# The hi parts of the input projection's weights cast by GpSimd, and the other arithmetic of the token mixing on VectorE and ScalarE

## The chip, the cores and the metric

The kernel runs on one core of a Trainium2 chip. The core has TensorE (matrix products; its weight loads are counted apart), VectorE and GpSimd (both elementwise), ScalarE (elementwise with a function), and DMA queues, most of them issued by SyncE. The metric is the device time of one execution in microseconds (us). A profile is one further execution, recorded by the hardware; its times can differ from the median by some tenths of a per cent.

## The reference, cut to what matters

A trunk of two layers over 1024 tokens of width 1024, in float32. Each layer has a norm with modulation, one input projection that two head groups share (differential attention, and an RWKV-7 recurrence), one output projection, and a mixture of experts:

```python
for l in range(DEPTH):
    h = rms_norm(x, norm1_g[l]) * (1.0 + sc1) + sh1
    proj = h @ w_in[l]
    q, k, v = ...                                   # group A: 4 heads, two softmax maps each
    attn_out = diff_attention(q, k, v, ...)
    rwkv_out = rwkv7_time_mix(proj[..., 3 * AW:], ...)   # group B: delta-rule state scan
    mixed = jnp.concatenate([attn_out, rwkv_out], axis=-1) @ w_out[l]
    x = x + gt1 * mixed
    h2 = rms_norm(x, norm2_g[l]) * (1.0 + sc2) + sh2
    x = x + gt2 * hier_moe(h2, ...)
return rms_norm(x, final_g)
```

## The kernel before, in words

Float32 products are made from three passes of TensorE's faster fp32r type. An operand is split in a hi part (rounded to fp32r) and a lo part (the operand less its hi), and the product is hi x hi + lo x hi + hi x lo. So each tile of weights costs a cast and a two-input subtract on some elementwise engine before TensorE can use it.

The stages of a layer follow one another, with their times in the profile: the first norm (to about 45 us in layer 0, 1385 to 1450 in layer 1); the mixing stage, `phase_a`, up to 905 and from 1450 to 2200; output projection and routing up to 1040 and 2320; the experts up to 1385 and 2690; the final norm.

In the mixing stage several generators are woven together:

- The input projection: `split_w` (L339) loads one of 25 weight tiles per layer by DMA into `wa_raw` (one buffer), casts it to `wa_hi`, subtracts to `wa_lo` (two buffers each). The first two tiles of a layer are cast by VectorE; the other 23 by ScalarE, through `wtile` (L439). `proj_cm` (L351) then makes 16 x 3 matmuls per tile for two halves of the tokens (L359 to L361).
- The recurrence: `rwkv_first` (L621), 4 pairs of heads by 4 quarters of the tokens. Its `chain` computes, mostly on VectorE, the decay `P` (L652), the products `bk` (L665, L666), and with GpSimd their scaled copies `bkb` (L669) and `arv[:, 0]` (L670, the identity scaled), each multiplied by the decay at the end of each chunk of 64 tokens, `pend`. TensorE multiplies them (`aa`, L681), transposes them (`tp`, L692), ScalarE copies the transposes out, VectorE masks `z` (L685). Then comes a triangular solve on VectorE (L748, L750), and the state scan `rwkv_back` (L866 on), whose bonus `b_bo` is a GpSimd product (L879), and `rwkv_last`, which norms a half and applies its scale and shift by three GpSimd operations (L931 to L933).
- The attention: `load_head` (L1073) splits q and k of a head, with ScalarE casts and GpSimd subtracts (L1092, L1097); then scores, softmax (`at_p`, L1178; the factors L1185, L1186; the difference L1187), transposes (L1196) and `at_o` (L1205).
- `out_weights` (L1220): 8 tiles of the output projection's weights per layer, each multiplied by the gate (VectorE, L1232), cast by ScalarE (L1233), its lo part subtracted by GpSimd (L1234).

The order on each engine is not the written one: a scheduler with its own model of durations takes the recorded instructions and lays each engine's row out, and the weaving adds due times. Each engine then runs its row in order. So an instruction that waits holds everything behind it on its engine.

Of the kernel before, what the change touches and what calls it, by code (L numbers as in the profile page):

```python
# [10 lines left out]
F32 = mybir.dt.float32  # L11
# [3 lines left out]
AF = mybir.ActivationFunctionType  # L15
OP = mybir.AluOpType
# [36 lines left out]
class Trunk:  # L53
# [285 lines left out]
    def split_w(self, wp, l, i, eng=None):  # L339

        nc = self.nc
        raw = wp.tile([128, NK, 128], F32, name="wa_raw", tag="wa_raw", bufs=1)
        nc.sync.dma_start(raw, self.a["w_in"][l, i])
        hi = wp.tile([128, NK, 128], F32R, name="wa_hi", tag="wa_hi")
        lo = wp.tile([128, NK, 128], F32R, name="wa_lo", tag="wa_lo")
        (eng or nc.vector.tensor_copy)(hi, raw)  # L346
        nc.gpsimd.tensor_tensor(lo, raw, hi.bitcast(F32), op=OP.subtract)  # L347
        return hi, lo


# [68 lines left out]
    def phase_a(self, l, x_src, psum, here, there):  # L419

        nc, a, tc = self.nc, self.a, self.tc
# [3 lines left out]
        wp, wl1, wk = self.wA, self.wl1, self.wk  # L425
# [11 lines left out]
                                   *(self.modulation(j, range(12), wpool, work, psum, 2) for j in range(1, L)))  # L437

        def wtile(c0):  # L439
            return self.split_w(wp, l, c0 // 128, eng=nc.scalar.copy)  # L440

        def lora():
            l1 = ring()
# [177 lines left out]
    def rwkv_first(self, hp, rp, ep, psum, krv, l2, w_up, a_up, sp):  # L621

        nc = self.nc
# [20 lines left out]
        def chain(q):  # L644
            k, r, v = (x[:, H * q:H * q + H] for x in krv)
# [3 lines left out]
            arv, bkb, bk = tl("arv", [128, 4, 4, 64]), tl("bkb", [128, 2, 4, 64]), tl("bk", [128, 2, 4, 64])  # L649
# [15 lines left out]
            nc.vector.tensor_mul(bk[:, 0], v3(ta), v3(u))  # L665
            nc.vector.tensor_mul(bk[:, 1], v3(th), v3(u))  # L666
            nc.scalar.copy(arv[:, 3], v3(v))
            for j in range(2):
                nc.gpsimd.tensor_tensor(bkb[:, j], bk[:, j], pend.to_broadcast([128, 4, 64]), op=OP.mult)  # L669
            nc.gpsimd.tensor_tensor(arv[:, 0], self.id2[:, None, :].to_broadcast([128, 4, 64]), pend.to_broadcast([128, 4, 64]), op=OP.mult)  # L670
            return arv, bkb, bk, rk

        def products(q, bk, arv, z):
# [190 lines left out]
    def rwkv_back(self, hp, q, t, pool, psum):  # L864
# [10 lines left out]
        if r == 0:  # L875
            self.bo = pool.tile([128, 4, 128], F32, name="b_bo", tag="b_bo")
            self.yh = pool.tile([128, 4, 128], F32, name="b_y", tag="b_y", bufs=2)
        bs = self.bsum[:, hp, 2 * q:2 * q + 2].rearrange("p t h -> p (t h)").unsqueeze(2).to_broadcast([128, 4, 64])
        nc.gpsimd.tensor_tensor(self.bo[:, r:r + 2].rearrange("p t (h n) -> p (t h) n", h=2), e[:, 1].rearrange("p t (h n) -> p (t h) n", h=2),  # L879
                                bs, op=OP.mult)  # L880
        hs = [slice(64 * h, 64 * h + 64) for h in range(2)]
        first = 0
# [33 lines left out]
    def rwkv_last(self, hp, half, y, bo, pool, psum):  # L916
# [11 lines left out]
        nc.vector.tensor_tensor(y3, y3, rs.unsqueeze(2).to_broadcast([128, 8, 64]), op=OP.mult)  # L928
        cs = slice(128 * hp, 128 * hp + 128)
        lnx = self.lnx  # L930
        nc.gpsimd.tensor_tensor(y, y, lnx[:, 0].unsqueeze(1).to_broadcast([128, 4, 128]), op=OP.mult)  # L931
        nc.gpsimd.tensor_tensor(bo, bo, lnx[:, 1].unsqueeze(1).to_broadcast([128, 4, 128]), op=OP.add)
        nc.gpsimd.tensor_tensor(y, y, bo, op=OP.add)  # L933

        def gate():
            ps = psum.tile([128, 4, 128], F32, name="rb_gt", tag="rb")
# [136 lines left out]
    def load_head(self, h):  # L1073
# [11 lines left out]
        for j, m, x in ((1, 0, tile("q0", F32)), (1, 1, tile("q1", F32)), (0, 0, tile("v", F32)), (0, 1, stage.tile([128, T], F32, name="st", tag="st"))):  # L1085
            for r in halves:
                nc.sync.dma_start(x[r], self.heads[h, j][halves[m]])
            if j:
                ks.append(tile(f"k{m}"))
                kl.append(tile(f"l{m}"))  # L1090
                nc.scalar.copy(ks[m], x)
                nc.gpsimd.tensor_tensor(kl[m], x, ks[m].bitcast(F32), op=OP.subtract)  # L1092
            else:
                dst = tile(f"q{m}")
                qs.append(dst)
                nc.scalar.copy(dst, x)
                nc.gpsimd.tensor_tensor(dst[64:128], x[64:128], dst[64:128].bitcast(F32), op=OP.subtract)  # L1097
        v = tile("v", F32).rearrange("p (t n) -> p t n", n=128)
        self.stacks[h] = (qs, ks, kl, v)
        nc.sync.dma_start(v, self.heads[h, 2])  # L1100
# [119 lines left out]
    def out_weights(self, l, k, wp, gate, keep):  # L1220
# [10 lines left out]
                      for n in names[2 * k:2 * k + 2])  # L1231
        nc.vector.tensor_tensor(raw, raw, gate, op=OP.mult)  # L1232
        nc.scalar.copy(hi, raw)  # L1233
        nc.gpsimd.tensor_tensor(lo, raw, hi.bitcast(F32), op=OP.subtract)  # L1234
        self.wo[k] = hi, lo

    def open_output(self, l, x_src, side):
# [736 lines left out]
```

## Time and profile before

| | us |
|---|---|
| Three timed runs | 2727.2, 2728.67, 2737.83 |
| Median | 2728.67 |
| The profiled execution: its time, its span | 2742.43, 2740.6 |
| TensorE busy in the span | 2400.2 |
| VectorE busy | 1836.7 |
| ScalarE busy | 1131.5 |
| GpSimd busy | 711.9 |

The mean granted clock of TensorE in that execution is 0.912 of full. An engine counts as busy while it runs an instruction, and also while an instruction that has started stands still for some other engine; such a stretch shows as a duration longer than the form's usual one. Idle time is put down to the instruction whose end came last before the waiting one could start.

### The profile page before, as it was taken

The numbers are of one execution on the slowest core, as the hardware profiler recorded it, in microseconds if no ns is written. First come the engines' busy times: TensorE is split into PE (matmuls) and PEld (weight loads), VectorE is DVE, ScalarE is ACT, GpSimd is POOL, SyncE is SP. The second block draws the span as 40 slices with busy tenths as digits, with TensorE's granted clock in tenths as the row PEclk, the third lists the DMA queues.
The fourth block names the chain that finished last, engine by engine and source line by source line (L and its number), as shares of the span: only waits on it lengthen the run. The fifth ranks groups of instructions, "written<-read, shape, count | busy, mean of one in ns | idle before, by whom it ended". The sixth has DMA issues, their size and how long they took to land. (4 is left out here: it accounts for less than half of the span.)

```text
span 2740.6 us, 45306 instructions
## 1 busy us (share of the span) xinstructions
PE 2400.2 (88%) x17313; PEld 1836.5 (67%) x17313; DVE 1836.7 (67%) x3803; ACT 1131.5 (41%) x2020; POOL 711.9 (26%) x525
## 2 busy tenths in 40 slices
PE   5998989898979969999959888889986897999992
PEld 3676657687767866777737666667765786677771
DVE  3358875464658477877753689974648847787775
ACT  4333332244345225555544333324426422455552
POOL 4122221313141013333311222323314200233330
PEclk7999988798979979999979989889988897999996
DMA  8476675534272258999851434355426224899985
GB/s 286 159 233 222 177 218 155 155 115 132 88 218 70 96 193 303 355 336 368 309 213 47 155 107 150 113 153 156 136 76 204 73 89 180 303 384 352 335 311 200
DMA packets 262787, 542.68 MB, mean 198 GB/s; under 512 B 76376, under 2 KB 180768, under 8 KB 232608
## 3 DMA queue, kind: packets, MB, share of 16 engines
q1 hardware_dynamic: 234560, 484.61, 52.6%
q0 software_dynamic: 23376, 40.99, 4.0%
q10 hardware_dynamic: 4624, 14.06, 1.4%
q8 instruction: 142, 2.33, 0.4%
q14 instruction: 85, 0.70, 0.1%
HBM read 459.29 MB, written 120.09 MB: 211 GB/s over the span
## 5 line engine op out<-in xcount | busy, mean ns | idle before, releaser
L1618 DVE TENSOR_TENSOR w_lo<-w_gu,w_hi 128x2048 fp32r<-128x2048 f32 x134 | 306.4, 2287 | 69.1 <-ACT w_hi L1617 68.8
L1617 ACT CAST w_hi<-w_gu 128x2048 fp32r<-128x2048 f32 x134 | 255.7, 1908 | 211.0 <-PE h_ps L1670 204.3
L359 PE MATMUL pj<-hh,wa_hi 128*128 128x512 f32 x800 | 338.2, 423 | 2.1 <-DVE bsum L711 0.7
L361 PE MATMUL pj<-hh,wa_lo 128*128 128x512 f32 x800 | 328.1, 411 | 4.3 <-POOL wa_lo L347 4.3
L360 PE MATMUL pj<-hl,wa_hi 128*128 128x512 f32 x800 | 329.7, 412 | 1.2 <-DVE hl L336 1.1
L1698 POOL DMA_INDIRECT yd<-yo,idx_s x70 | 183.5, 2621 | 289.9 <-DVE yo L1695 275.1
L1709 PE MATMUL y_ps<-w_d,hT 128*128 128x512 f32 x560 | 252.3, 593 | 3.4 <-ACTq L1770 2.4
L1669 PE MATMUL h_ps<-w_hi,xT_hi 128*128 128x512 f32 x560 | 243.0, 434 | 4.4 <-ACT xT_hi L1653 4.4
L1670 PE MATMUL h_ps<-w_hi,xT_lo 128*128 128x512 f32 x560 | 222.5, 397 | 2.5 <-DVE xT_lo L1654 2.5
L1671 PE MATMUL h_ps<-w_lo,xT_hi 128*128 128x512 f32 x560 | 222.4, 397 | 0.0
L347 POOL TENSOR_TENSOR wa_lo<-wa_raw,wa_hi 128x1024 fp32r<-128x1024 f32 x50 | 123.4, 2468 | 296.2 <-ACT wa_hi L346 235.3
L359 PEld LDWEIGHTS pj<-hh,wa_hi 128*128 128x128 f32 x800 | 156.2, 195 | 42.9 <-issue 7.5
L361 PEld LDWEIGHTS pj<-hh,wa_lo 128*128 128x128 f32 x800 | 155.9, 195 | 41.1 <-POOL wa_lo L347 5.7
L360 PEld LDWEIGHTS pj<-hl,wa_hi 128*128 128x128 f32 x800 | 156.0, 195 | 37.1 <-DVE hl L336 4.4
L1709 PEld LDWEIGHTS y_ps<-w_d,hT 128*128 128x128 f32 x560 | 100.9, 190 | 104.8 <-issue 100.4
L1637 POOL DMA_INDIRECT xg<-h2d,idx_g x70 | 75.8, 1082 | 232.8 <-PE xT_ps L1645 204.2
L1669 PEld LDWEIGHTS h_ps<-w_hi,xT_hi 128*128 128x128 f32 x560 | 107.3, 192 | 38.0 <-issue 11.5
L1670 PEld LDWEIGHTS h_ps<-w_hi,xT_lo 128*128 128x128 f32 x560 | 107.3, 192 | 36.6 <-DVE th L1661 11.5
L1654 DVE TENSOR_TENSOR xT_lo<-xT_ps,xT_hi 128x1024 fp32r<-128x1024 f32 x70 | 85.7, 1225 | 65.6 <-ACT xT_hi L1653 65.6
L1671 PEld LDWEIGHTS h_ps<-w_lo,xT_hi 128*128 128x128 f32 x560 | 106.9, 191 | 23.0
L1178 ACT ACTIVATE at_p<-at_s,at_mx 128x256 f32<-128x256 f32 (+7 forms) x128 | 95.0, 743 | 64.4 <-DVE at_mx L1176 63.8
L748 DVE TENSOR_TENSOR sv_m<-sv_t,sv_n 64x31 f32<-64x31 f32 (+15 forms) x248 | 103.1, 416 | 26.4 <-DMA sv_n<-sp_z 21.8
(436 smaller groups left out, 5227.3 us busy)
## 6 DMA issues: line engine op xcount, KB each, us to landing
w_gu<-in_moe_w_gu SPq DMA_DIRECT2D x140, 1024.0 KB
w_d<-in_moe_w_down SPq DMA_DIRECT2D x70, 1024.0 KB
ada_w<-in_ada_w SPq DMA_DIRECT2D x80, 512.0 KB
wa_raw<-in_w_in SPq DMA_DIRECT2D x50, 512.0 KB
sp_z<-z SPq DMA_DIRECT2D x32, 768.0 KB
b_zz<-sp_z SPq DMA_DIRECT2D x32, 512.0 KB
cy<-yd SPq DMA_DIRECT2D x16, 1024.0 KB
qkv<-qst SPq DMA_DIRECT2D x48, 256.0 KB
```

Of the source, the lines that this page charges most:

```text
L347: nc.gpsimd.tensor_tensor(lo, raw, hi.bitcast(F32), op=OP.subtract)
L359: nc.tensor.matmul(ps, hi[:, k, :], self.hh[k][:, sl], start=(k == 0), stop=False)
L360: nc.tensor.matmul(ps, hi[:, k, :], self.hl[k][:, sl], start=False, stop=False)
L361: nc.tensor.matmul(ps, lo[:, k, :], self.hh[k][:, sl], start=False, stop=(k == NK - 1))
L748: eng.tensor_tensor(t3, tt[:, 0:j + 1, j].unsqueeze(2).to_broadcast([64, j + 1, 31 - j]), nt[:, j, j + 1:32].unsqueeze(1).to_broadcast([64 ...
L1617: self.nc.scalar.copy(hi, raw)
L1618: eng.tensor_tensor(lo, raw, hi.bitcast(F32), op=OP.subtract)
L1669: nc.tensor.matmul(ph, hi[:, k, :], whi[:, k % 4, :], start=(k == 0), stop=False)
L1670: nc.tensor.matmul(ph, lo[:, k, :], whi[:, k % 4, :], start=False, stop=False)
L1671: nc.tensor.matmul(ph, hi[:, k, :], wlo[:, k % 4, :], start=False, stop=(k == NK - 1))
L1698: st = nc.gpsimd.indirect_dma_start(out=self.yd, out_offset=bass.IndirectOffsetOnAxis(ap=self.idx_s[:, e:e + 1], axis=0), in_=yos[e % 2], ...
L1709: nc.tensor.matmul(po[:, 512 * half:512 * half + 512], hT[:, k, :], w[:, k, 512 * half:512 * half + 512], start=(k == 0), stop=(k == 1))
```

## The change

The 46 casts of `wa_hi` that ScalarE made go to GpSimd. All two-input arithmetic that GpSimd did from the first norm to the experts leaves it: the subtracts of `wa_lo` (50), of the heads' q and k (32) and of the output weights (16), the bonus products (32) and the scale and shift of the state's output (48) go to VectorE; the three scaled copies of each chain (32 groups) become eight ScalarE activations of 128x2x64 or 128x64 with a scale per partition. GpSimd keeps memsets, its DMA issues and the experts' gathers and scatters.

```diff
@@ split_w
-        nc.gpsimd.tensor_tensor(lo, raw, hi.bitcast(F32), op=OP.subtract)
+        nc.vector.tensor_tensor(lo, raw, hi.bitcast(F32), op=OP.subtract)
@@ phase_a, wtile
-            return self.split_w(wp, l, c0 // 128, eng=nc.scalar.copy)
+            return self.split_w(wp, l, c0 // 128, eng=nc.gpsimd.tensor_copy)
@@ rwkv_first, chain
-            for j in range(2):
-                nc.gpsimd.tensor_tensor(bkb[:, j], bk[:, j], pend.to_broadcast([128, 4, 64]), op=OP.mult)
-            nc.gpsimd.tensor_tensor(arv[:, 0], self.id2[:, None, :].to_broadcast([128, 4, 64]), pend.to_broadcast([128, 4, 64]), op=OP.mult)
+            for i in range(4):
+                nc.scalar.activation(bkb[:, :, i], bk[:, :, i], AF.Copy, scale=pend[:, i])
+            for i in range(4):
+                nc.scalar.activation(arv[:, 0, i], self.id2, AF.Copy, scale=pend[:, i])
@@ rwkv_back
-        nc.gpsimd.tensor_tensor(self.bo[:, r:r + 2]...
+        nc.vector.tensor_tensor(self.bo[:, r:r + 2]...
@@ rwkv_last
-        nc.gpsimd.tensor_tensor(y, y, lnx[:, 0].unsqueeze(1).to_broadcast([128, 4, 128]), op=OP.mult)
-        nc.gpsimd.tensor_tensor(bo, bo, lnx[:, 1].unsqueeze(1).to_broadcast([128, 4, 128]), op=OP.add)
-        nc.gpsimd.tensor_tensor(y, y, bo, op=OP.add)
+        nc.vector.tensor_tensor(y, y, lnx[:, 0].unsqueeze(1).to_broadcast([128, 4, 128]), op=OP.mult)
+        nc.vector.tensor_tensor(bo, bo, lnx[:, 1].unsqueeze(1).to_broadcast([128, 4, 128]), op=OP.add)
+        nc.vector.tensor_tensor(y, y, bo, op=OP.add)
@@ load_head
-                nc.gpsimd.tensor_tensor(kl[m], x, ks[m].bitcast(F32), op=OP.subtract)
+                nc.vector.tensor_tensor(kl[m], x, ks[m].bitcast(F32), op=OP.subtract)
-                nc.gpsimd.tensor_tensor(dst[64:128], x[64:128], dst[64:128].bitcast(F32), op=OP.subtract)
+                nc.vector.tensor_tensor(dst[64:128], x[64:128], dst[64:128].bitcast(F32), op=OP.subtract)
@@ out_weights
-        nc.gpsimd.tensor_tensor(lo, raw, hi.bitcast(F32), op=OP.subtract)
+        nc.vector.tensor_tensor(lo, raw, hi.bitcast(F32), op=OP.subtract)
```

The scheduler lays out new rows. Lines of the changed kernel from L669 on are one higher than before. On GpSimd, in the first recurrent stage of layer 0, the row before had the chains' scaled copies and the subtracts in turn (`id` is the identity):

```order
L670 TENSOR_TENSOR arv<-id_93,P 128x256
L669 TENSOR_TENSOR bkb<-bk,P 128x256 x2
L347 TENSOR_TENSOR wa_lo<-wa_raw,wa_hi 128x1024
L670 TENSOR_TENSOR arv<-id_93,P 128x256
L669 TENSOR_TENSOR bkb<-bk,P 128x256 x2
```

and in the changed kernel it has the casts, between the DMA issues for the modulation's biases:

```order
L229 DMA ada_bias<-in_ada_b 32x4x128 x4
L346 CAST wa_hi<-wa_raw 128x1024 x4
L229 DMA ada_bias<-in_ada_b 32x4x128 x4
L346 CAST wa_hi<-wa_raw 128x1024 x3
L229 DMA ada_bias<-in_ada_b 32x4x128 x4
```

What stood between two casts on ScalarE now stands between nothing else than such issues on GpSimd.

On ScalarE, one group of the chain in the same stage, before (`avt` and `z` are copies of the transposes `tp`, `th` and `ta` open the next chain, `P` and `u` are its exponentials):

```order
L346 CAST wa_hi<-wa_raw 128x1024
L375 ACTIVATE krv<-pj,omu_336 128x511
L376 ACTIVATE krv<-pj,carry,omu_336 128x1
L693 COPY avt<-tp 128x512
L663 COPY arv<-kn 128x4
L667 COPY arv<-krv 128x256
L693 COPY z<-tp 128x512
L641 ACTIVATE th<-zwa,hbias_338 128x256
L642 ACTIVATE ta<-zwa,hbias_338 128x256
```

and of the changed kernel:

```order
L375 ACTIVATE krv<-pj,omu_336 128x511
L376 ACTIVATE krv<-pj,carry,omu_336 128x1
L694 COPY avt<-tp 128x512
L663 COPY arv<-kn 128x4
L667 COPY arv<-krv 128x256
L671 ACTIVATE arv<-id_93,P 128x64 x4
L694 COPY z<-tp 128x512
L669 ACTIVATE bkb<-bk,P 128x2x64 x4
L641 ACTIVATE th<-zwa,hbias_338 128x256
L642 ACTIVATE ta<-zwa,hbias_338 128x256
```

The cast is gone from the group; the eight scaled copies stand around the copy of the transposes, four of them right ahead of `th`. That they stand so is the case in 12 of the 32 groups.

On VectorE, at a place in the first recurrent stage of layer 0 of the changed kernel, where the last products of a chain (`bk`) are followed by the first steps of a solve (`sv_m`, `sv_t`):

```order
L665 TENSOR_TENSOR bk<-ta,u 128x256
L666 TENSOR_TENSOR bk<-th,u 128x256
L241 TENSOR_TENSOR modE<-ada_ps,ada_bias 128x128
L749 TENSOR_TENSOR sv_m<-sv_t,sv_n 64x31
L347 TENSOR_TENSOR wa_lo<-wa_raw,wa_hi 128x1024
L751 TENSOR_TENSOR sv_t<-sv_t,sv_m 64x31
```

The subtract of a weight tile now stands between two dependent steps of the solve, where VectorE's row before had none. In the first norm of layer 0 another one stands between the steps L107 and L108 of the Newton iteration for the reciprocal root.

## Rows read from the trace of the kernel before

**Rows 1.** Page: busy us of each engine, share of the span, instructions.

```profile
PE 2400.2 (88%) x17313; PEld 1836.5 (67%) x17313; DVE 1836.7 (67%) x3803; ACT 1131.5 (41%) x2020; POOL 711.9 (26%) x525
```

**Rows 2.** Stretches: length, busy PE/PEld/DVE/ACT/POOL (instructions), PEclk, DMA, GB/s.

```profile
200.00:400.00 200.00, 175.24 (x1510) 125.67 (x1508) 164.28 (x409) 70.52 (x139) 51.26 (x52) 0.93 0.69 212
...
750.00:905.00 155.00, 131.53 (x807) 109.67 (x800) 106.40 (x234) 78.38 (x193) 44.91 (x26) 0.87 0.48 152
...
1500.00:1850.00 350.00, 306.15 (x2659) 235.45 (x2658) 278.91 (x740) 122.48 (x265) 90.00 (x81) 0.91 0.43 134
...
2050.00:2200.00 150.00, 111.93 (x650) 95.19 (x648) 118.61 (x239) 85.42 (x220) 45.47 (x25) 0.87 0.43 131
```

**Rows 3.** Timeline, GpSimd and VectorE: start, length, instruction, [idle before].

```profile
34.97 2.34 POOL L347 TENSOR_TENSOR wa_lo<-wa_raw,wa_hi 128x1024 fp32r<-128x1024 f32 x1 [20.91 <-DVE rs_u_n L107]
34.98 2.34 DVE L108 TENSOR_TENSOR rs_u_n<-rs_u_n,rs_y_n 128x2 f32<-128x2 f32 x1
...
1568.33 2.37 POOL L347 TENSOR_TENSOR wa_lo<-wa_raw,wa_hi 128x1024 fp32r<-128x1024 f32 x1 [12.21 <-ACT wa_hi L346]
...
1569.00 1.74 DVE L748 TENSOR_TENSOR sv_m<-sv_t,sv_n 64x31 f32<-64x31 f32 x1 [4.59 <-DMA sv_n<-sp_z]
...
1570.78 0.18 DVE L750 TENSOR_TENSOR sv_t<-sv_t,sv_m 64x31 f32<-64x31 f32 x1
...
2173.25 2.38 POOL L1234 TENSOR_TENSOR wo_x<-wo_raw,wo_3at_v 128x1024 fp32r<-128x1024 f32 x1 [1.16 <-ACT wo_3at_v L1233]
2173.55 3.01 DVE L1212 SCALAR_TENSOR_TENSOR at_ob<-at_ob,rs_y_sub,subg 128x128 f32<-128x128 f32 x4
```

**Rows 4.** What TensorE waited for, 200 to 400: us, times, longest.

```profile
PE ada_ps L238 <- DMA ada_w<-in_ada_w: 10.9, 9, 2.1
PE aa L681 <- DVE arv L664: 4.2, 2, 2.7
PE tp L692 <- DVE z L685: 4.0, 4, 2.7
PE aa L681 <- DVE bk L665: 2.3, 1, 2.3
```

**Rows 5.** The same, 1500 to 1850.

```profile
PE zwa L638 <- ACT ta L642: 6.7, 1, 6.7
PE rb_m L851 <- DVE b_sb L895: 5.2, 4, 4.5
...
PE pj L361 <- POOL wa_lo L347: 4.3, 4, 1.5
...
PE rb_y L902 <- DVE b_sb L895: 0.2, 1, 0.2
```

**Rows 6.** ScalarE's groups: count | busy, mean ns | idle before, releasers.

```profile
L346 ACT CAST wa_hi<-wa_raw 128x1024 fp32r<-128x1024 f32 x46 | 48.1, 1047 | 106.8 <-PE pj L360 93.0 <-issue 7.1 <-DMA wa_raw<-in_w_in 3.7
```

**Rows 7.** The same, GpSimd.

```profile
L347 POOL TENSOR_TENSOR wa_lo<-wa_raw,wa_hi 128x1024 fp32r<-128x1024 f32 x50 | 123.4, 2468 | 296.2 <-ACT wa_hi L346 235.3 <-DVE sv_t L750 23.4 <-DVE rs_u_n L107 20.9
...
L669 POOL TENSOR_TENSOR bkb<-bk,P 128x256 f32<-128x256 f32 x64 | 44.7, 717 | 30.1 <-PE tp L692 14.4 <-DVE bk L666 11.9 <-DVE bk L665 2.8
...
L1631 POOL MEMSET xg<- 128x1024 f32 x4 | 3.8, 951 | 189.0 <-DVE h L1367 186.3 <-DVE h L1368 2.7
```

**Rows 8.** The same, VectorE.

```profile
L1792 DVE TENSOR_TENSOR xm<-xm,cy 128x1024 f32<-128x1024 f32 x16 | 19.5, 1221 | 0.2
...
L666 DVE TENSOR_TENSOR bk<-th,u 128x256 f32<-128x256 f32 x32 | 14.0, 437 | 0.0
...
L923 DVE TENSOR_TENSOR b_y<-b_y,b_st 128x512 f32<-128x512 f32 x16 | 11.1, 691 | 0.5
```

**Rows 9.** What TensorE waited for, 2050 to 2200.

```profile
PE at_s L1171 <- ACT at_p L1178: 12.2, 10, 2.8
```

**Rows 10.** Timeline, ScalarE, in the attention of layer 1.

```profile
2069.64 0.36 ACT L1206 ACTIVATE at_ob<-at_o,at_rec 128x128 f32<-128x128 f32 x1
...
2069.89 0.47 ACT L1178 ACTIVATE at_p<-at_s,at_mx 128x256 f32<-128x256 f32 x1
```

More of the change, by code (lines that the diff above doesn't have):

```diff
@@ L878, in rwkv_back @@
         bs = self.bsum[:, hp, 2 * q:2 * q + 2].rearrange("p t h -> p (t h)").unsqueeze(2).to_broadcast([128, 4, 64])
-        nc.gpsimd.tensor_tensor(self.bo[:, r:r + 2].rearrange("p t (h n) -> p (t h) n", h=2), e[:, 1].rearrange("p t (h n) -> p (t h) n", h=2),
+        nc.vector.tensor_tensor(self.bo[:, r:r + 2].rearrange("p t (h n) -> p (t h) n", h=2), e[:, 1].rearrange("p t (h n) -> p (t h) n", h=2),
                                 bs, op=OP.mult)
```

## The prediction

> **What bounds the kernel now.** The first view is busy time by engine [rows 1]: TensorE 2400 us of the span (88%), VectorE 1837 (67%), ScalarE 41%, GpSimd 26%. TensorE sets the time, so an edit elsewhere counts only where TensorE waits for it. The second view cuts the span by stage [rows 2]. The stretch with the recurrent chains of layer 0 (200 to 400 us) has VectorE busy 164.3 of 200 (82%) and TensorE idle 24.8; that of layer 1 (1500 to 1850) has VectorE busy 278.9 of 350 (80%) and TensorE idle 43.9. There VectorE is nearly full. In the attention tails (750 to 905, 2050 to 2200) TensorE idles 23.5 and 38.1 us.
>
> The third view, the timeline, says what fills VectorE [rows 3]. At 1568.33 GpSimd starts a weight subtract of 2.37 us; a VectorE operation on 64x31 elements starts at 1569.00 and takes 1.74 us, ending with GpSimd's, while its neighbour of equal size takes 0.18. I compared each VectorE duration with the lower quartile of its form. 163 instructions are over it by more than 60 ns, by 140 us in all; 158 of them (139 us) overlap a two-input GpSimd operation. The first of them (34.98, 2.34 us for a 128x2 operation) and the last (2173.55, 3.01 us for four 128x128) are in [rows 3]. By stretch: 23.3 us in 200 to 400, 39.8 in 1500 to 1850, 38.7 in the two attention tails, the rest where VectorE has room. So 23.3 of 164 and 39.8 of 279 us of "busy" are stalls.
>
> The Trainium skill's page "SBUF — State Buffer", section "Who interferes with whom", says the same and adds something against the change: a VectorE operation with two SBUF inputs and a GpSimd operation that reads SBUF exclude each other, and whoever issues first holds the port for its whole length. The rows at 1568 agree. By that rule the casts, which read SBUF too, still block VectorE; the sum below prices that from rows.
>
> The fourth view, what TensorE waited for, gives the ceiling. In 200 to 400, three waits ended by VectorE make 10.5 us; the 10.9 us behind the modulation weights are a DMA's [rows 4]. In 1500 to 1850, 14 lines ended by VectorE (5.2 us the first, 0.2 the last) make 25 us, GpSimd's subtract 4.3, ScalarE's `ta` 6.7 [rows 5].
>
> **Part by part.** Durations come from the profiled execution: span 2740.6, its own time 2742.4, which is 0.5% above the median 2728.7. I sum against 2742.4 and scale.
>
> *Hi casts to GpSimd.* GpSimd loses all its two-input work (about 400 us) and takes 46 one-input casts of 128x1024. The trace has no such cast. Bounds: a memset of that shape, which only writes, takes 0.95 us; the two-input subtract 2.47 on average, 2.34 unhindered [rows 3, 7]. I take 1.2, near the memset, since one stream is read instead of two. The Trainium skill's "GPSIMD Engine Reference", section "Engine selection", puts one-input work at about line rate; by that nothing in the sum moves. ScalarE loses 46 x 1.047 = 48 us [rows 6].
>
> *Subtracts, bonus and scale products to VectorE.* A two-input 128x1024 there takes 1.22 us, 128x512 0.69, 128x256 0.43 [rows 8]. 98 of the first (50 weight tiles of w_in, 32 of the heads, 16 of w_out; half-height ones last as long), 48 of the second, 32 of the third: 120 + 33 + 14 = 167 us on VectorE against 140 us of stalls that go. Over the whole kernel VectorE gets no lighter; what matters is where.
>
> - *200 to 400*: 8 subtracts come, 9.8 us. Stalls of 23.3 go. New stalls by 8 casts of 1.2 us: the present stall is 23.3 us per 44.8 us of GpSimd arithmetic (of its 51.3 busy us there), 0.52, so 5.0. Net relief 23.3 - 9.8 - 5.0 = 8.5 us.
> - *1500 to 1850*: 13 subtracts and a few small products, 23.1 us. 39.8 go; new stalls 13 x 1.2 x 39.8/88 (88 of its 90.0 busy us are arithmetic) = 7.0. Net 9.7.
> - VectorE is busy 80 to 82% there [rows 2], so I let 0.8 of 18.2 reach the end: **-14 us**. Bounds: 0, and -33 if nearly all VectorE-ended waits (10.5 + 25) vanish. With a cast at 0.95 the net grows by 2.5, at 2.34 it shrinks by 11.
> - *Clock*: granted 0.93 and 0.91 of full there, 0.87 in the tails [rows 2]; shorter idles return a little: **-5** (0 to -10).
> - *Attention tails*: stalls of 38.7 go, subtracts and norm products of 41.6 come; equal. But the subtracts are placed between operations rather than falling on the softmax chain, where TensorE waits 12.2 us for `at_p` [rows 9]: **-3** (-8 to +5).
> - *Elsewhere* (400 to 750, 1850 to 2050): the remaining 92 us come and 38 us of stalls go. TensorE's streams of projection matmuls hide that as long as it falls off the chains; with that cover gone, 54 would show.
> - *First norm*: the small Newton step falls from 2.34 to 0.2 us, but a 1.2 us subtract stands ahead of it in VectorE's row: **-1**.
>
> *Chain products to ScalarE.* 32 groups lose three GpSimd products (0.72 us each for the 64 `bkb`, [rows 7]) and get eight small scaled copies on ScalarE. Pitch: a scaled ScalarE activation of 128x128 starts at 2069.64 and the next instruction at 2069.89, so 0.25 us [rows 10]; 256 x 0.25 = 64 us, against 48 removed. ScalarE is 35% busy in both stretches [rows 2], so its sum is covered. Its order isn't: in 12 of 32 groups the four `bkb` copies stand right ahead of the `th` activation that opens the next chain, about 1 us each, and they wait for `bk`, VectorE's last step of the chain. A third to a half shows: **+5** (0 to +25: the 6.7 us wait for `ta` [rows 5] is what such a delay looks like).
>
> Sum: -14 - 5 - 3 - 1 + 5 = -18, so 2724 for the profiled execution, times 2728.7/2742.4: **2711 us**.
>
> **The rivals.**
>
> *Stalls are worth more.* If all waits ended by VectorE in the two stretches (35 us) and GpSimd's 4.3 go, the tails give 8 and the clock 10, the gain is 57: 2672. For it: the stalls fall on tiny operations in dependent chains, where each is latency and not only load. Against it: the 25 us are spread over 14 lines, 1.8 us a line, and new work comes into the same queue.
>
> *It washes out.* VectorE's total rises from 1837 - 140 to 1837 - 140 + 167 plus the casts' stalls; if the scheduler's order puts the subtracts on the chains as often as the stalls fell on them, the relief is zero and only ScalarE's +5 and the clock's -5 remain: 2729. For it: the equal sums above.
>
> *VectorE's queue stops behind the casts* (slower). Before, a subtract that was early waited on GpSimd, whose queue holds little else. Now it stands in VectorE's in-order row inside the solve and the chains, waits for GpSimd's cast, which waits for TensorE to leave the buffer, and everything behind it waits too: the solve, `z`, `bk`. ScalarE's casts waited 93.0 us for TensorE, 2.0 per cast [rows 6]; with the cast's own 1.2 that is 3.2 per tile. For the 21 tiles of the two full stretches, half of 67 us charged gives +34, less the 18: +16, 2745. It decides once a tile costs 18/21 = 0.9 us more than its 1.22. With the ScalarE turn at its bound this ends at about 2750. Against it: in the order the subtract stands well behind its cast, and the casts run ahead on a nearly empty GpSimd.
>
> That the change doesn't do what it says can be left out: the order shows all arithmetic but the casts and memsets gone from GpSimd in these stages.
>
> **How the numbers follow.** 2711 with its own range 2697 to 2724: 0.42. Worth more, around 2672: 0.15. Washes out, 2715 to 2740: 0.20. Slower, 2742 to 2765: 0.23. 0.5% (13.6 us) is about what a measurement of this kernel can tell from no change, so under 2715 is faster and above 2742 slower. A quarter of the first case lies above 2715: faster 0.32 + 0.15 = 0.47; same 0.10 + 0.20 = 0.30; slower 0.23. The range runs from 2676 to 2750; it leaves out about half of the second case below and, with the bounds of cast and ScalarE order, some half of the slow one above, 0.19 together.
>
> **What would show it.** Right: VectorE's small operations in the chains back to their undisturbed length; VectorE's busy share in 200 to 400 and 1500 to 1850 at 75 to 80%; TensorE's idle there down by 8 and 10 us; a GpSimd cast near 1.2 us. Wrong: casts near 2.3 us; VectorE idle "released by GpSimd `wa_hi`" inside the chains or TensorE waiting for `wa_lo` from VectorE; waits for `ta` or `th` grown beyond 15 us; the tails longer than before.

## The result and the profile after

The changed kernel takes 2702.6 us (2693.8 to 2706.7) against 2731.4 for the kernel before on the same chips: a ratio of 0.9888, with a 95% interval of 0.9855 to 0.9922, some 29 us. The forecast was 2711, in a range of 2676 to 2750. The direction came out, and the size within the range, though 29 is more than the 18 that were forecast. The place did not come out, and the rest of this document is about that.

The two profiled executions lie 48.6 us apart (spans of 2740.6 and 2692.0), more than the medians. The one of before is 11 us above its kernel's median, the one of after 9 us below. So a stage's length in one profile is good to some microseconds only, and below I rest on lengths that repeat over several kernels.

Busy time by engine, after, the counterpart of [rows 1]:

```profile
PE 2377.0 (88%) x17313; PEld 1822.3 (68%) x17313; DVE 1865.6 (69%) x3981; ACT 1155.2 (43%) x2230; POOL 369.9 (14%) x297
```

VectorE is 29 us busier, and still the kernel is faster. The groups of the split weights, after (count | busy, mean ns | idle time ahead of them and what ended it), GpSimd's cast, VectorE's subtract, and the attention's factor `at_g`:

```profile
L346 POOL CAST wa_hi<-wa_raw 128x1024 fp32r<-128x1024 f32 x46 | 56.6, 1230 | 826.9 <-PE pj L360 699.9 <-issue 44.5 <-DMA b_aa<-sp_z 32.7
...
L347 DVE TENSOR_TENSOR wa_lo<-wa_raw,wa_hi 128x1024 fp32r<-128x1024 f32 x50 | 60.8, 1216 | 0.3
...
L1187 DVE SCALAR_TENSOR_TENSOR at_g<-at_sum,nlam,at_rec 128x1 f32<-128x1 f32 x64 | 14.6, 228 | 0.9
```

The cast takes 1.23 us on average (1.2 was assumed), the subtract 1.22, and VectorE waits 0.3 us in all for 50 subtracts. Half of the 46 casts take 1.05 us or less; the mean is drawn up by casts that stand still, one of them for most of 5.31 us, in which VectorE ran a row of mostly two-input operations without a gap:

```profile
372.66 5.31 POOL L346 CAST wa_hi<-wa_raw 128x1024 fp32r<-128x1024 f32 x1 [7.93 <-PE pj L360]
```

It ended 1.0 us after the first operation of that row that reads from PSUM (`modE`, L241, at 376.98) had started. So VectorE seems to hold GpSimd up as well; this is one case. `at_g` is a 128x1 operation that nobody edited; before, its mean was 446 ns for 228 after:

```profile
L1186 DVE SCALAR_TENSOR_TENSOR at_g<-at_sum,nlam,at_rec 128x1 f32<-128x1 f32 x64 | 28.5, 446 | 1.3
```

By the measure used in the prediction (durations over the lower quartile of their form by more than 60 ns), VectorE's stalls fall from 140 to 18 us, in 29 instructions, 25 of which overlap a cast. This is one, in the timeline of after (start, length, instruction):

```profile
239.54 1.57 POOL L346 CAST wa_hi<-wa_raw 128x1024 fp32r<-128x1024 f32 x1 [21.41 <-PE pj L360]
...
240.20 1.18 DVE L749 TENSOR_TENSOR sv_m<-sv_t,sv_n 64x247 f32<-64x247 f32 x1
...
241.63 0.40 DVE L751 TENSOR_TENSOR sv_t<-sv_t,sv_m 64x247 f32<-64x247 f32 x1
```

`sv_m` started during the cast and lasted until 0.27 us after it; its twin of the same size took 0.40. So the casts block VectorE as the subtracts did: 18 us for 56.6 us of casts is 0.32 us per us, before it was 140 for the 403 us of its two-input operations, 0.35. They are half as long, and there are fewer of them.

The same stretches as in [rows 2], after (length, busy time of TensorE, its weight loads, VectorE, ScalarE, GpSimd, granted clock, DMA share, GB/s):

```profile
200.00:400.00 200.00, 183.58 (x1601) 132.94 (x1594) 152.20 (x418) 85.29 (x216) 20.82 (x20) 0.96 0.68 211
...
1500.00:1850.00 350.00, 314.08 (x2818) 244.01 (x2816) 271.12 (x774) 143.74 (x377) 19.00 (x22) 0.91 0.49 147
```

VectorE's share is 76 and 77%, TensorE's idle time 16.4 and 35.9 us, 8 us less each. But fixed stretches don't hold the same work after a change: TensorE runs 1601 instructions in the first where it had 1510. One stage can be cut so that TensorE's work in it is the same in all kernels: the attention tail, from the end of the projection's last L359 matmul to the last `at_o`, with 557 TensorE instructions in layer 0 and 649 in layer 1 (to a record or two). Before:

```profile
771.00:894.50 123.50, 101.28 (x557) 85.60 (x557) 92.37 (x184) 72.58 (x179) 44.20 (x25) 0.83 0.47 147
...
2053.90:2202.50 148.60, 110.28 (x649) 94.04 (x648) 115.32 (x226) 85.55 (x219) 45.47 (x25) 0.87 0.42 129
```

and after:

```profile
764.40:876.80 112.40, 93.22 (x557) 81.40 (x556) 94.01 (x202) 72.33 (x179) 0.94 (x2) 0.89 0.52 163
...
2029.50:2154.80 125.30, 104.10 (x649) 89.86 (x648) 108.24 (x244) 84.77 (x219) 0.97 (x2) 0.92 0.50 154
```

The tails are shorter by 11.1 and 23.3 us, 34 of the 48.6 between the two profiles. For these I had forecast 3, and no more than 8. Of the 34, 20 is idle time of TensorE (length less busy: 22.2 to 19.2, 38.3 to 21.2), and 14 is that the same matmuls run faster (101.3 to 93.2, 110.3 to 104.1), with the granted clock up from 0.83 to 0.89 and from 0.87 to 0.92 of full (means over the stretch of its two levels, 1.2 and 2.4 GHz). By these means the lower level was granted for some 42 us before and 25 after in layer 0, and for 39 and 20 in layer 1.

The two layers differ. In layer 1 TensorE's waits that VectorE ended fall from 12.7 us,

```profile
PE mT_ps L1294 <- DVE br L1281: 4.5, 1, 4.5
PE at_t L1196 <- DVE at_p L1187: 2.8, 2, 1.8
PE at_t L1196 <- DVE rs_u_sub L107: 2.8, 1, 2.8
PE n_cb L1280 <- DVE n_tmp L1277: 2.6, 1, 2.6
```

to 0.2:

```profile
PE at_t L1197 <- DVE at_p L1188: 0.2, 1, 0.2
```

In layer 0 the same sum is 7.3 us before and 6.2 after, TensorE idles only 3.0 us less, and 8.1 of the 11.1 us are the clock. Why the clock stays up there isn't shown; it does so in every kernel below that has VectorE's subtracts and ScalarE's casts in its tails.

### The profile page after: what moved, and what is told of

It is laid out like the page before. It is cut to its first block, busy times and chain, and to the rows that moved or that the text cites. A ratio compares the mean times of both kernels' runs of the same rounds, so it can differ in the third digit from the quotient of the medians.

```text
span 2692.0 us, 45342 instructions
## 1 busy us (share of the span) xinstructions
PE 2377.0 (88%) x17313; PEld 1822.3 (68%) x17313; DVE 1865.6 (69%) x3981; ACT 1155.2 (43%) x2230; POOL 369.9 (14%) x297
## 5 line engine op out<-in xcount | busy, mean ns | idle before, releaser
L359 PE MATMUL pj<-hh,wa_hi 128*128 128x512 f32 x800 | 336.8, 421 | 0.1
L359 PEld LDWEIGHTS pj<-hh,wa_hi 128*128 128x128 f32 x800 | 155.6, 195 | 40.4 <-issue 9.1
L346 POOL CAST wa_hi<-wa_raw 128x1024 fp32r<-128x1024 f32 x46 | 56.6, 1230 | 826.9 <-PE pj L360 699.9
L1696 DVE SCALAR_TENSOR_TENSOR yo<-y_ps,wsl,gt 128x1024 f32<-128x1024 f32 x70 | 89.9, 1284 | 38.2 <-PE y_ps L1710 38.2
L1177 DVE TENSOR_REDUCE at_mx<-at_s 128x1 f32<-128x256 f32 (+7 forms) x128 | 95.7, 753 | 22.3 <-PE at_s L1175 21.3
```

Source lines behind the costliest of these rows:

```text
L359: nc.tensor.matmul(ps, hi[:, k, :], self.hh[k][:, sl], start=(k == 0), stop=False)
L1177: nc.vector.tensor_reduce(mx, ps[:, 0:n], axis=AX.X, op=OP.max, negate=True)
```

## The experiments

### One part of the change undone

The hi casts back to ScalarE:

```diff
-            return self.split_w(wp, l, c0 // 128, eng=nc.gpsimd.tensor_copy)
+            return self.split_w(wp, l, c0 // 128, eng=nc.scalar.copy)
```

> The changed kernel with the 46 hi casts back on ScalarE, so that GpSimd has no arithmetic at all in the mixing stages. Theory (stalls): the gain of 30 us is VectorE freed of GpSimd's two-input operations; the casts' own stalls are small (29 VectorE instructions, 18 us over the whole changed kernel against 140 before), so VectorE's stalls fall to about 0, ScalarE's busy time rises by 48 us, and the time stays within 0.4% of the changed kernel: 2695 to 2712, ratio to before 0.987 to 0.993. Rival (ScalarE): the gain is ScalarE freed of the casts; then all of it goes back and the time is 2725 to 2740, ratio 0.998 or more, since ScalarE now has the chain products as well.

Measured: 2701.5 us, ratio 0.9891 (0.9865 to 0.9917): no difference to the changed kernel. The rival that the gain is ScalarE's falls. The trace of this run shows something else, in VectorE's group of the subtracts:

```profile
L347 DVE TENSOR_TENSOR wa_lo<-wa_raw,wa_hi 128x1024 fp32r<-128x1024 f32 x50 | 61.0, 1220 | 45.3 <-ACT wa_hi L346 42.2 <-DMA lam_v<-in_attn_lambda 2.6 <-DMA b_aa<-sp_z 0.2
```

With ScalarE's casts VectorE's row stands 42 us for `wa_hi`; with GpSimd's, 0.3. That is the wait of my slower rival, and giving the cast to GpSimd removes it. It cost the whole kernel nothing that can be measured, but 18 us of casts' stalls went with it, so the run doesn't price the wait alone.

The 50 subtracts of the weights back to GpSimd:

```diff
-        nc.vector.tensor_tensor(lo, raw, hi.bitcast(F32), op=OP.subtract)
+        nc.gpsimd.tensor_tensor(lo, raw, hi.bitcast(F32), op=OP.subtract)
         return hi, lo
```

> The changed kernel with the 50 subtracts of the projection's weights (wa_lo) back on GpSimd, its casts there as well. Theory (stalls): these subtracts make the larger part of the stalls in the chain stretches; VectorE loses 61 us of work and gets some 50 us of stalls on small dependent operations, and the time rises by 8 to 20 us, to 2710 to 2722, ratio 0.993 to 0.997. Rival (load): VectorE's load is what counts, so taking 61 us of work off it is worth more than the stalls and the time falls below 2697, ratio under 0.987. Rival (ScalarE): nothing changes, ratio 0.988 to 0.991.

Measured: 2740.6 us, ratio 1.0042 (1.0022 to 1.0062). The sign is that of the stalls, the size (38 us over the changed kernel) is twice what I allowed. VectorE's stalls rise from 18 to some 84 us. The rival that VectorE's load counts most falls, and so does the one that nothing changes. The stretch from the first `aa` to the last step of the solve, 311 us in layer 1 of the changed kernel, is this here:

```profile
1509.60:1844.90 335.30, 293.69 (x2522) 223.83 (x2521) 260.68 (x710) 132.44 (x354) 47.59 (x31) 0.87 0.42 132
```

The chain's products back to GpSimd (the two hunks of `chain` reversed):

> The changed kernel with the chain's three scaled products back on GpSimd (96 operations of 0.7 to 0.9 us). Theory (stalls): they run next to VectorE's chain operations and stall these for some 25 us in all, of which a third reaches the end, while ScalarE is freed of 75 us of small activations that stand ahead of th; net loss 0 to 8 us: 2702 to 2711, ratio 0.989 to 0.993. Rival (ScalarE order): the eight activations per group cost more than the stalls, and the time falls by 5 us or more, ratio under 0.987.

Measured: 2718.4 us, ratio 0.9962 (0.9942 to 0.9982): 16 us more than the changed kernel, where one theory had 8 or less and the other a gain. ScalarE's wait ahead of `th`, after and in this run:

```profile
L641 ACT ACTIVATE th<-zwa,hbias 128x256 f32<-128x256 f32 x32 | 15.0, 469 | 23.6 <-DVE bk L666 15.4 <-PE zwa L639 8.1
```

```profile
L641 ACT ACTIVATE th<-zwa,hbias 128x256 f32<-128x256 f32 x32 | 15.2, 475 | 45.4 <-PE zwa L639 29.4 <-DVE bk L666 15.9
```

The eight small activations that I had feared ahead of `th` don't make it wait longer for `bk`: 15.4 us with them, 15.9 without. The run also brings stalls back on VectorE (18 to some 46 us), so its 16 us are not the price of the copies alone.

The heads and the output weights back to GpSimd:

```diff
-                nc.vector.tensor_tensor(kl[m], x, ks[m].bitcast(F32), op=OP.subtract)
+                nc.gpsimd.tensor_tensor(kl[m], x, ks[m].bitcast(F32), op=OP.subtract)
-                nc.vector.tensor_tensor(dst[64:128], ...)
+                nc.gpsimd.tensor_tensor(dst[64:128], ...)
-        nc.vector.tensor_tensor(lo, raw, hi.bitcast(F32), op=OP.subtract)
+        nc.gpsimd.tensor_tensor(lo, raw, hi.bitcast(F32), op=OP.subtract)
         self.wo[k] = hi, lo
```

> The changed kernel with the subtracts of the heads (32) and of the output weights (16) back on GpSimd. Theory (stalls): in the attention tails removed stalls and added work were forecast equal, so the time moves by no more than 6 us: 2698 to 2709, ratio 0.987 to 0.992. Rival (tails): the tail of layer 1, which is 23 us shorter in the profile of the changed kernel, owes this to the subtracts having left GpSimd; then 10 us or more come back, ratio 0.992 or more.

Measured: 2720.6 us, ratio 0.9969 (0.9948 to 0.999): 18 us more, the rival's answer. Its tails, cut as above:

```profile
774.50:898.30 123.80, 102.64 (x557) 87.93 (x557) 95.14 (x186) 71.95 (x179) 42.56 (x23) 0.82 0.48 148
...
2031.90:2181.40 149.50, 112.83 (x649) 96.65 (x648) 115.96 (x228) 84.82 (x219) 42.30 (x23) 0.86 0.43 129
```

Length, TensorE's busy time and clock are those of before, to a few per cent. The tails are 36 us longer than in the changed kernel and the time only 18: not all of a tail's length reaches the end. The stretches from the first `aa` to the tail are 10 longer in layer 0 and 18 us shorter in layer 1 in this run, which is why I don't take one profile's stretches for the kernel's.

### One part alone

Heads and output weights alone on VectorE, in the kernel before:

```diff
-                nc.gpsimd.tensor_tensor(kl[m], x, ks[m].bitcast(F32), op=OP.subtract)
+                nc.vector.tensor_tensor(kl[m], x, ks[m].bitcast(F32), op=OP.subtract)
-                nc.gpsimd.tensor_tensor(dst[64:128], ...)
+                nc.vector.tensor_tensor(dst[64:128], ...)
-        nc.gpsimd.tensor_tensor(lo, raw, hi.bitcast(F32), op=OP.subtract)
+        nc.vector.tensor_tensor(lo, raw, hi.bitcast(F32), op=OP.subtract)
         self.wo[k] = hi, lo
```

> The kernel before with one part of the change alone: the subtracts of the heads (32) and of the output weights (16) on VectorE. Theory (stalls, and the tails pay most): the two attention tails fall to the lengths they have in the changed kernel, 112 and 125 us against 124 and 149, because the 43 us of stalls there sit on the softmax chain; the time falls by 15 to 30 us, ratio 0.989 to 0.9945. Rival (the order as a whole): the tails are shorter only in the changed kernel's order; then the ratio is 0.996 to 1.002.

Measured: 2707.5 us, ratio 0.991 (0.9887 to 0.9934). These 48 subtracts, of 274 operations that the change moves besides the casts, give 23 us (by the medians) to 25 us (by the ratio) of the 29 by themselves. The tails:

```profile
758.30:870.60 112.30, 92.25 (x558) 79.62 (x557) 92.51 (x200) 72.22 (x179) 4.31 (x9) 0.89 0.52 162
...
2039.80:2168.80 129.00, 108.75 (x648) 93.70 (x648) 106.68 (x242) 84.72 (x219) 4.32 (x9) 0.88 0.48 149
```

The weights' subtracts alone on VectorE (the edit of `split_w` alone):

> The kernel before with the 50 wa_lo subtracts alone on VectorE, hi casts on ScalarE, chain products on GpSimd as before. Theory (stalls): some 50 us of stalls go, mostly in the recurrent chains, 61 us of work come; the tails stay at 124 and 149 us and the time falls by 5 to 20 us, ratio 0.9925 to 0.998. Rival (load): VectorE's row gets longer for nothing, ratio 1.000 to 1.006. The run before this, with these subtracts moved back, rose by 38 us; if the parts add up, this one falls by as much, ratio 0.986.

Measured: 2729.5 us, ratio 0.9996 (0.9977 to 1.0016): nothing. By the same measure its stalls are 100 us against 149 for before (taken over both traces, so that 149 stands here for 140 above): a third of the stalls is gone, and no time. VectorE's row waits for ScalarE's cast:

```profile
L347 DVE TENSOR_TENSOR wa_lo<-wa_raw,wa_hi 128x1024 fp32r<-128x1024 f32 x50 | 65.1, 1302 | 45.9 <-ACT wa_hi L346 44.7 <-DMA sp_z<-z 0.3 <-DMA b_aa<-sp_z 0.3
```

Here 45 us of waits and 65 us of work stand against 49 us of stalls. What each of them is worth at the end, this run doesn't tell.

### The stalls without the work

All 98 lo parts filled with zeros by a GpSimd memset, in the kernel before:

```diff
-        nc.gpsimd.tensor_tensor(lo, raw, hi.bitcast(F32), op=OP.subtract)
+        nc.gpsimd.memset(lo.bitcast(F32), 0.0)
         return hi, lo
```

(and likewise in `load_head` and `out_weights`)

> The kernel before in which GpSimd fills all lo parts that it computed (projection weights, heads, output weights) with zeros by memset and does not subtract; the products with lo parts then add nothing, and the work of these 98 subtracts is left out. GpSimd only writes there, and VectorE gets no work. Theory (stalls come from GpSimd's reads): the stalls that these subtracts made, 100 of some 149 us, go without anything in their place, tails fall to 112 and 125 us, and the time is at or below the changed kernel's: 2680 to 2705, ratio 0.981 to 0.990. Rival (any GpSimd work stalls VectorE): the memsets last 0.95 us against 2.34, so 60 us of stalls go, and the ratio is 0.990 to 0.995. Rival (the order): no clear change, ratio 0.996 or more.

Measured: 2653.5 us, ratio 0.9706 (0.9682 to 0.9731), 77 us below the kernel before and more than any theory had. It bounds what stalls and subtracts are worth together, but it isn't the stalls alone: a weight tile's memset waits neither for the load nor for the cast, so the lo part is early and the load buffer is free sooner. Which share is which wasn't tried. In its timeline a memset and the VectorE operations beside it:

```profile
134.68 0.95 POOL L347 MEMSET wa_lo<- 128x1024 f32 x1 [12.97 <-PE pj L361]
134.82 0.69 DVE L502 SCALAR_TENSOR_TENSOR sq<-sq,kn 128x512 f32<-128x512 f32 x1 [0.70 <-ACT kn L501]
135.54 0.69 DVE L503 TENSOR_TENSOR sq<-sq,kn 128x512 f32<-128x512 f32 x1
...
157.87 0.95 POOL L347 MEMSET wa_lo<- 128x1024 f32 x1 [0.94 <-PE pj L361]
157.89 1.08 DVE L650 TENSOR_SCALAR th<-th 128x256 f32<-128x256 f32 x1 [2.02 <-ACT th L641]
158.90 0.28 DVE L655 TENSOR_SCALAR ta<-ta 128x256 f32<-128x256 f32 x1
```

The two-input operations keep their 0.69 us beside a memset; the one-input `th` waits it out. Of 42 VectorE operations with two inputs from SBUF that began under a memset alone, none was held up; of nine one-input copies, casts and scalings that read and write SBUF, all nine were (copies from PSUM and reductions never). Under GpSimd's two-input operations both kinds are held up; of those with two inputs from SBUF, 131 of 163 in the trace of before.

### Shorter pieces

Each of the 98 subtracts on GpSimd, as before, cut into eight of 128 columns:

```diff
-        nc.gpsimd.tensor_tensor(lo, raw, hi.bitcast(F32), op=OP.subtract)
+        for k in range(NK):
+            nc.gpsimd.tensor_tensor(lo[:, k], raw[:, k], hi[:, k].bitcast(F32), op=OP.subtract)
         return hi, lo
```

> The kernel before with each of GpSimd's 98 subtracts (projection weights, heads, output weights) cut into eight of 128 columns; nothing else changed. Theory (a VectorE operation is held up for the rest of the GpSimd instruction that runs when it starts): a hold is then at most 0.3 us instead of 2.34, so the roughly 100 us of stalls from these subtracts fall to 20 to 50, VectorE gets no work in exchange, and the time comes near the run without the subtracts: 2665 to 2705, ratio 0.976 to 0.990. Rival (the stalls go by GpSimd's busy time, 0.35 us per us): the stalls stay near 149 us, in more and smaller ones, and the ratio is 0.996 to 1.005.

Measured: 2714.5 us, ratio 0.9939 (0.9922 to 0.9955), between the two. Stalls fall from 149 to 102 us, not to 20 to 50, and come in 381 instructions in place of 194. The timeline of the attention in this run shows why (`x9` is a run of nine):

```profile
780.70 3.76 POOL L1094 TENSOR_TENSOR at_l<-at_q,at_k 128x128 fp32r<-128x128 f32 x9
...
782.06 0.37 DVE L107 SCALAR_TENSOR_TENSOR rs_u_sub<-rs_v_sub,rs_y_sub 128x4 f32<-128x4 f32 x1
782.46 0.37 DVE L108 TENSOR_TENSOR rs_u_sub<-rs_u_sub,rs_y_sub 128x4 f32<-128x4 f32 x1
782.87 0.38 DVE L109 SCALAR_TENSOR_TENSOR rs_y_sub<-rs_u_sub,rs_y_sub 128x4 f32<-128x4 f32 x1
783.28 0.38 DVE L107 SCALAR_TENSOR_TENSOR rs_u_sub<-rs_v_sub,rs_y_sub 128x4 f32<-128x4 f32 x1
```

The two engines take turns: a VectorE operation of 0.16 us, a piece of GpSimd's, and so on, at 0.41 us a pair. A chain of small operations is held up at every link instead of once. GpSimd pays as well: its pieces take 0.53 us on average, 4.3 us a tile against 2.47.

Heads and output weights on VectorE, and the weights' subtracts in pieces:

> The kernel before with the subtracts of the heads and output weights on VectorE, as in the run with that part alone (ratio 0.991), and the 50 wa_lo subtracts on GpSimd in eight pieces each. Theory (holds last as long as the GpSimd instruction): the tails stay at 112 and 125 to 129 us and the chains lose some 35 us of stalls besides: 2675 to 2700, ratio 0.980 to 0.989, below the changed kernel. Rival (stalls by busy time): ratio 0.989 to 0.994, as without the pieces.

Measured: 2702.6 us, ratio 0.9895 (0.9869 to 0.992), no clear difference to the run without the pieces (0.991), although some 23 us of stalls are gone. That is the rival's ratio, but not its reason, which was that the stalls stay. Pieces on heads and output weights shortened the tails (121.0 and 136.4 us for 123.5 and 148.6); pieces on the projection's weights alone show no gain.

### More casts for GpSimd

The hi casts of the heads and of the output weights on GpSimd as well, in the changed kernel:

```diff
-                nc.scalar.copy(ks[m], x)
+                nc.gpsimd.tensor_copy(ks[m], x)
-                nc.scalar.copy(dst, x)
+                nc.gpsimd.tensor_copy(dst, x)
-        nc.scalar.copy(hi, raw)
+        nc.gpsimd.tensor_copy(hi, raw)
```

> The changed kernel with the hi casts of the heads' q and k (32) and of the output weights (16) on GpSimd too, off ScalarE. In the tails TensorE still waits for ScalarE (at_p, at_wt). Theory (stalls): a GpSimd cast of 1.23 us stalls VectorE at the rate measured in the changed kernel, 18 us of stalls for 57 us of casts, so 48 casts bring some 19 us, most of them in the tails, and ScalarE loses 50 us; the two nearly cancel: ratio 0.985 to 0.994. Rival (ScalarE is late in the tails): tails shorten below 110 and 120 us and the ratio falls under 0.985. Rival (every stall in the tails costs its length): tails 5 to 10 us longer each, ratio 0.993 to 0.997.

Measured: 2701.7 us, ratio 0.9882 (0.986 to 0.9903), the same as the changed kernel. The tails are longer again (127.5 and 132.6 us) with 6 us of stalls in each, though ScalarE has 14 to 15 us less to do there:

```profile
755.80:883.30 127.50, 94.45 (x557) 80.42 (x556) 100.86 (x202) 57.73 (x163) 25.17 (x23) 0.84 0.46 143
...
2034.50:2167.10 132.60, 104.73 (x649) 89.61 (x648) 113.62 (x244) 70.49 (x203) 24.57 (x23) 0.92 0.48 145
```

and the stretches from the first `aa` to the tail are 8 and 4 us shorter than in the changed kernel. In layer 0 stalls of 6 us aren't the whole reason. TensorE there waits once for 19.6 us, for the subtract of a head's q on VectorE. The q's cast is the last of a row on GpSimd and ends at 792.64; the subtract then stands in VectorE's row behind `g`, an operation of the second norm that waits for its own load:

```profile
PE at_s L1172 <- DVE at_q L1098: 19.6, 1, 19.6
...
791.60 1.04 POOL L1097 CAST at_q<-at_v 128x1024 fp32r<-128x1024 f32 x1
...
797.95 1.23 DVE L1255 SCALAR_TENSOR_TENSOR g<-g,n2g 128x1024 f32<-128x1024 f32 x1 [7.41 <-DMA n2g<-in_norm_g]
799.21 1.22 DVE L1098 TENSOR_TENSOR at_q<-at_v,at_q 64x1024 fp32r<-64x1024 f32 x1
```

In the changed kernel `g` waits 0.4 us there. So this run tells neither what the casts' stalls cost in that tail nor whether ScalarE's load matters in it: it took load off ScalarE and put other waits in its place.

### Is it the order?

The undone parts add up to 72 us (38, 16, 18, and 0 for the cast) where the whole is 29. The bonus products and the scale and shift (80 of the 274 operations) were never undone by themselves. So I changed the order alone, by writing the two groups of ScalarE copies in each chain the other way round:

> The changed kernel with the two groups of four scaled ScalarE copies of each chain written in the other order (identity first, then bkb); every instruction is the same, some 200 lines of TensorE's and ScalarE's rows stand elsewhere. Theory (parts): the time stays within 0.3% of the changed kernel, ratio 0.985 to 0.992. Rival (order): part of what the single parts cost when undone (16 to 38 us each, 76 together where the whole is 30) is only the luck of an order; then this moves by 8 us or more, ratio above 0.992 or below 0.985.

Measured: 2694.9 us, ratio 0.9856 (0.9834 to 0.9878), 8 us below the changed kernel's median, with intervals that overlap. It is the fastest of the complete kernels here, by an amount that I can't tell from nothing. This one reordering, of some 200 of TensorE's and ScalarE's rows, moved the time by 8 us, about the size that the rival asked for, though not clear of noise; the undone parts moved it by twice that and more, but they also reorder far more rows, so order isn't excluded for a part of their 16 to 38 us.

The last run puts both halves of the weights' split back, hi on ScalarE and lo on GpSimd, in the changed kernel:

> The changed kernel with both halves of the weights' split where they were before, hi on ScalarE and lo on GpSimd; chain copies, bonus, scale and shift, heads and output weights as changed. With lo alone moved back the time had risen by 38 us (ratio 1.004), more than its 65 us of returned stalls can pay at the third to a half that reached the end elsewhere. Theory A (cast and subtract one behind the other on GpSimd make it so slow): with the cast on ScalarE the time falls back to that of the run with heads and output weights alone, 2700 to 2715, ratio 0.988 to 0.994. Theory B (the chain's copies on ScalarE wait for a VectorE that is stalled, and hold ScalarE's row): it stays at 2728 to 2745, ratio 0.998 to 1.006. In between, both or the order.

Measured: 2723.9 us, ratio 0.9977 (0.9955 to 0.9999), in between. Cast and subtract in a row on GpSimd account for 17 of the 38 us; the other 21 stay. Against the run with heads and output weights alone (2707.5), this kernel has the chain's copies on ScalarE and the bonus, scale and shift on VectorE, and is 16 us slower. So those two parts, or the order that comes with them, cost time while GpSimd subtracts weights, and the first of them gains 16 us when it doesn't. Why the parts interact so stays open.

### The tails over all kernels

The length of the tails in us, layer 0 and 1, and VectorE's stalls in them:

| subtracts in the tails | kernels | layer 0 | layer 1 | stalls |
|---|---|---|---|---|
| on GpSimd | before; heads and weights undone; weights' lo alone on VectorE | 123.5, 123.8, 127.6 | 148.6, 149.5, 147.0 | 17 to 18 and 24 to 26 |
| on GpSimd in pieces | pieces | 121.0 | 136.4 | 12 and 12 |
| on VectorE | after and the seven others with ScalarE's casts there | 110.7 to 112.4 | 125.3 to 129.5 | 0 |
| on VectorE, casts on GpSimd | more casts | 127.5 (one wait of 19.6) | 132.6 | 6 and 6 |
| none, memsets | lo parts zero | 110.7 | 123.2 | 1 and 1 |

This is the one finding that repeats over all fourteen kernels: no kernel with GpSimd's subtracts in whole reaches 113 and 130, and none with VectorE's, and ScalarE's casts, misses it. That GpSimd's subtracts are slow, and so late for TensorE, is hardly the reason: TensorE's own waits for them in the tails of before are 0.7 us in all, and with the pieces, where a subtract takes 4.3 us in place of 2.5, the tails got shorter as the stalls got fewer. And VectorE's 16 subtracts a tail, 19.5 us of new work, cost nothing there that the kernel with memsets could show: 110.7 against 110.7 to 112.4, and 123.2 against 125.3 to 129.5.

## Why the prediction was right, and where it was wrong

The total was right: 2702.6 for 2711, inside the own range of the likeliest case. In part that is luck: the tails gave many times their term, while the weights' subtracts, most of the work behind the largest term, gave nothing alone. Point by point:

- *The cast at 1.2 us, its stalls at 12 us in the two full stretches.* 1.23 us and 9.9 us (3.6 and 6.3). Right in the mean; an undisturbed cast takes 1.04 us.
- *VectorE's stalls go and its total rises by 167 - 140 plus the casts' stalls.* That is 39 with 12 us of casts' stalls, 45 with the 18 measured. VectorE's instructions got 41 us longer together; its busy time, in which instructions that overlap count once, rose by 29. The shares of 75 to 80% and TensorE's idle time down by 8 and 10 us came as forecast (76 and 77%, 8.4 and 8.0).
- *-14 us from the chain stretches* (0.8 of 18.2 is 14.6). From the first `aa` to the last step of the solve the changed kernel needs 309 and 311 us in place of 330 and 329, but the projection that goes on behind has 10 and 13 us more left: together -16 in the two profiles. The size fits, yet the runs don't bear out its mechanism as simple as I had it: the weights' subtracts alone gave nothing, and moved back in the changed kernel they cost 38.
- *The attention tails, -3 us (-8 to +5).* This is the step that failed. I set 38.7 us of stalls against 41.6 us of added work and called it equal, with 3 us off because the subtracts are placed between operations. Both sizes hold roughly (43 us of stalls and some 38 of work in the tails as cut above), and so does the reason for the 3; its size doesn't, since the two aren't the same kind of time. The stalls fell on whichever VectorE operation started beside a subtract: some 16 of the 43 us on the softmax's factors and differences (`at_g` 446 ns for 228, the row above), 15 on the norm behind it, the rest elsewhere. That the subtracts stand in time in which VectorE would have waited is argued, from its busy share of 75 and 78% in these tails and from the run with memsets. The runs showed 11 and about 20 us in place of 3, and 23 to 25 us for this part alone. In layer 1 TensorE's waits for VectorE went; in layer 0 most of the gain is the clock, and that part of the cause stays open.
- *The clock, -5 (0 to -10).* In the tails alone the same matmuls ran 14 us faster, at a granted clock of 0.89 and 0.92 for 0.83 and 0.87. Mis-sized: the tails, where most of it came, were set at 3 us.
- *The chain's copies on ScalarE, +5 (0 to +25).* No run shows such a cost: `th` waited 15.4 us for `bk` with the copies ahead of it, 15.9 without. Undone, the copies cost 16 us, but stalls come back with that, so the sign of this term alone isn't shown.
- *The first norm, -1.* The first `pj` starts 2.6 us sooner in layer 0 and, counted from the end of the first layer's tail, 1.3 in layer 1, but in layer 0 the first `aa` comes 4 us later.
- *The slower rival, VectorE's queue behind the casts.* The wait is real, 42 and 45 us in the two runs with ScalarE's casts and VectorE's subtracts, and it is 0.3 us in the changed kernel: GpSimd, with nothing else to do, has the cast ready. The forecast had it behind GpSimd's casts, at +16 us; it comes behind ScalarE's. Its price isn't shown alone: the runs with and without it take 2701.5 and 2702.6 us, but the first also lacks the casts' stalls. In that rival's sum ScalarE's term at its bound (+25 for +5) gives 2765, as in the chances, and not about 2750.

The Trainium skill's page "SBUF — State Buffer", section "Who interferes with whom", says that a VectorE operation with two SBUF inputs contends with a GpSimd operation that reads SBUF and not with one that only writes it. The casts' stalls agree with it (0.32 us per us), and so does the run with memsets, where none of 42 was held up by a write. The section also says that VectorE's copies, casts and scalings by a scalar contend with GpSimd when they run in a mode that uses two ports; all nine were held up by memsets, though no run here shows the mode itself.

## What to carry to other kernels

A stall and added work of equal length needn't cancel. In these tails 43 us of stalls went, some 38 us of work came, and they got 34 us shorter in the profiles: the stall falls on whatever operation is next, the work can stand in a gap. So price a stall by what waits for the stalled operation and added work by the idle time around it, and do so stage by stage, with TensorE's waits at hand. The same move gave 23 to 25 us alone in the tails and nothing alone in the projection's weights, although both took stalls away. And parts don't add up: the weights' subtracts gave nothing on top of the kernel before and cost 38 us when they were moved back in the changed one.

## What was not expected of the hardware

- GpSimd's subtract cut into eight pieces doesn't free VectorE: the two alternate at 0.41 us a pair, VectorE's 128x4 operations take 0.37 for 0.16 us, and GpSimd's 128x128 pieces 0.53 us on average.
- VectorE seems to hold GpSimd up as well: a cast that takes 1.04 us undisturbed lasted 5.31 beside a row of VectorE operations (one case).
- A GpSimd memset leaves VectorE's two-input operations alone (0 of 42 held up) and holds up its one-input operations (nine of nine, 0.29 us becoming up to 1.08).
- TensorE's clock gave back much of the time: of 34 us in the tails, 20 were less idle time and 14 the same matmuls in less time, at a mean granted clock of 0.89 and 0.92 for 0.83 and 0.87; in layer 0 the clock was 8 of 11 us.
